# Two-layer hybrid encoder: fp32r weight halves made by casting and adding transfers instead of a raw copy and two engines

## The chip, the cores and the metric

The kernel runs on one core of a Trainium2 chip. The metric is the device time of one execution in microseconds; the profile shows one such execution, with TensorE (PE; PEld is its weight load), VectorE (DVE), ScalarE (ACT), GpSimd (POOL), SyncE (SP) and the 16 DMA engines of the core.

## The reference

Sizes: 512 tokens, width 1024, two layers, MLP width 2816, a memory of 256 tokens. Cut to what matters here, every layer is a chain of matrix products with weights that are read once:

```python
for i in range(DEPTH):
    h = rms_norm(x, attn_norm[i])
    if i % 2 == 0:
        proj = h @ w_in_diff[0]          # 1024 x 2560: q, k, v, memory queries
        mix = diff_attention(...)
    else:
        proj = h @ w_in_gla[0]           # 1024 x 2576: q, k, v, gates, memory queries
        mix = gla_attention(...)
    cross = memory_cross_attention(mem_q, mem, ..., w_mem_kv[i], ...)   # 1024 x 512
    x = x + concat(mix, cross) @ w_out[i]                              # 1024 x 1024
    h = rms_norm(x, ffn_norm[i])
    u = h @ w_up[i]                                                    # 1024 x 5632
    c = causal_depthwise_conv3(u) + conv_b
    a, g = split(c, 2)
    x = x + (silu(g) * a) @ w_down[i]                                  # 2816 x 1024
```

All inputs and outputs are fp32.

## The kernel before

The big products run on TensorE in the type fp32r, which holds fewer bits than fp32. So that the result keeps its accuracy, each fp32 operand is held as two fp32r tiles: `hi`, the operand rounded to fp32r, and `lo`, the rest (operand minus `hi`). A product is then three matmuls: hi by hi, hi by lo, lo by hi. Activations are split where they are made (`xsh`, `xsl`, `midh`, `midl`). The weights are split on the chip as they arrive, and the change is about that.

The host packs all weights into `wpack`, one block after another in the order of use. A block is 128 partitions by up to 1024 columns (`WTILE`), 512 KB when full. Several blocks make a piece (`_pieces`, `_blocks`). A projection piece of 512 output columns has four blocks (two row tiles of the weight in each); an "up" piece ("ua" or "ug": 256 columns of the one or the other half of `w_up`) has two; a "down" piece has three, in the second half of the MLP two and a half.

`make_piece` brings one piece: for each block SP loads it into one of three `raw` buffers (L207), ACT copies it with rounding into a `whi` tile (L200), and DVE subtracts that from the raw block into a `wlo` tile (L201). `whi` and `wlo` are rings of `WB` = 5 tiles each. `weights(key)` hands out the piece that comes next and makes sure that one piece ahead of it has been ordered. The first piece (`raw0` to `raw3`) and the second are brought in the opening section by loads written out by hand (L373, and `second`), with the same split.

TensorE's order is the order in which the program is written. The order on ACT, DVE, POOL and SP is chosen by a scheduler when the kernel is built, outside the opening section; each engine then works through its own list in that order and waits on semaphores.

Around the weights: `gemm` (L250 to L252) computes a projection, for each of four groups of 128 tokens over all blocks of the piece, and hands its units to the queue `F` (class `Filler`), which slips them between the steps of attention. `product` (L267 to L269) computes 128 output columns for all 512 tokens with the weights as the stationary operand. In `ffn` a round takes one "ua" and one "ug" piece and runs four products: ua, ug, ua, ug. In the first layer a product takes the row tiles in the order 4, 0, 5, 1, 6, 2, 7, 3 (from `tiles`), so that it reads both of its blocks by turns; in the second layer in the order 0 to 7. After each product DVE multiplies by the row scale (L1017), ACT and DVE do the convolution (L1019 to L1021), the silu and the split (L1047 to L1051). POOL has little to do: it fills corners of `bt` and the first columns of `u` (memsets, L606, L1005), and adds sums of squares (L335).

Of the kernel before, what the change touches and what calls it, by code (L numbers as in the profile page):

```python
# [10 lines left out]
F32 = mybir.dt.float32  # L11
# [3 lines left out]
ALU = mybir.AluOpType  # L15
# [13 lines left out]
WTILE = 1024  # L29
HALVES = (6, 5)  # L30
XS = 36
WB = 5
FA, FB = 3.0, 1.2
K8 = tuple(range(KT))
C4 = tuple(range(4))
# [93 lines left out]
def trunk(ctx, tc, x_t, mem_t, wpack, cols_a_d, cols_d, conv_d, gate_d, rel_bias, diff_lambda, consts, onehot, out):  # L129
    nc = tc.nc  # L130
    mm = nc.tensor.matmul
    V, A, G = nc.vector, nc.scalar, nc.gpsimd
# [3 lines left out]
    wp = ctx.enter_context(tc.tile_pool(name="wp", bufs=2))  # L136
# [5 lines left out]
    def bank(tag):  # L142
        return ps.tile([128, 512], F32, name=f"ps_{tag}", tag=tag)

    def xtile():
        return xs.tile([128, S], F32, name="xt", tag="xs", bufs=XS)

    def split_tiles(pool=None, tag="xs", bufs=XS):
        pool = pool or xs
        return (pool.tile([128, S], F32R, name=tag + "h", tag=tag, bufs=bufs),  # L150
                pool.tile([128, S], F32R, name=tag + "l", tag=tag, bufs=bufs))
# [4 lines left out]
    def blk(b, w=128):  # L156
        return slice(w * b, w * b + w)
# [39 lines left out]
    at = [0]  # L197

    def split_weights(c, raw, hi, lo):
        A.copy(hi[:, c], raw[:, c])  # L200
        V.tensor_sub(lo[:, c], raw[:, c], hi[:, c].bitcast(F32))  # L201

    def raw_tile():
        return wp.tile([128, WTILE], F32, name="raw", tag="raw", bufs=3)

    def load_raw(raw, n):
        nc.sync.dma_start(raw[:, :n], wpack[at[0], :, :n])  # L207
        at[0] += 1
        return raw

    def make_piece(raws=None):
        parts = []
        for i, (_, _, kk, _, w) in enumerate(blocks[len(made)]):
            n = len(kk)
            raw = load_raw(raw_tile(), n * w) if raws is None else raws[i]
            hi, lo = (wp.tile([128, WTILE], F32R, name=t, tag=t, bufs=WB) for t in ("whi", "wlo"))
            split_weights(slice(0, n * w), raw, hi, lo)
            parts += [(hi[:, blk(j, w)], lo[:, blk(j, w)]) for j in range(n)]
        made.append(parts)

# [2 lines left out]
    def weights(key):  # L223
        i = used[0]
        assert plan[i][0] == key, (plan[i][0], key)
        while len(made) < min(i + 2, len(plan)):
            make_piece()
        used[0] += 1
        parts, made[i] = made[i], None
        return parts  # L230

    def split(hi, lo, src, gain):
        A.activation(hi, src, AF.Copy, scale=gain)
        V.scalar_tensor_tensor(lo, src, gain, hi.bitcast(F32), op0=ALU.mult, op1=ALU.subtract)  # L234
# [76 lines left out]
    def bias_rows(rb, oh, bs):  # L311
        for c in (slice(0, 512), slice(512, 640)):
            n = c.stop - c.start
            p = bank("lg")
            mm(p[:6, :n], rb, oh[:, c], start=True, stop=True)
            V.tensor_copy(bs[c.start // 512], p[:6, :n])
# [14 lines left out]
    def squares(src, acc, eng=V):  # L331
        sq = xtile()
        A.activation(sq, src, AF.Square)
        if acc[0] is not None:
            eng.tensor_add(sq, sq, acc[0])  # L335
        acc[0] = sq

    def token_rsqrt(tag, sq, nb, y, on_dve=False):
        p = bank(tag)
        for b in range(nb):  # L340
            mm(p[:, b:b + 1], sq[:, blk(b)], ones[:, 0:1], start=True, stop=True)
        return rsqrt(p[:, :nb], nb, 1.0 / D, on_dve, y=y)

    def small_vectors():
        for c in (c_dq, c_mq(0), c_mq(1)):
            V.tensor_scalar_mul(c, c, 0.125)
        V.tensor_scalar_mul(c_do, c_do, 1.0 - LAM_INIT)
        for t in range(3):
            V.tensor_scalar_mul(c_go(t), c_go(t), 0.5)
        lam(lv, xtile()[:, 0:128].rearrange("p (a b) -> p a b", a=2))  # L350
# [3 lines left out]
    with tc.tile_pool(name="ini", bufs=1) as ip, tc.manual_schedule(engines={E.Activation, E.DVE, E.Pool, E.SP}):  # L354
        idle = ip.tile([128, 512], F32, name="idle")
        rb = ip.tile([32, 6], F32, name="rb")
        oh = ip.tile([32, 640], F32, name="oh")
        bs = xtile()[:6], xtile()[:6, :128]
        lv = xtile()[:, :256]
        G.memset(idle, 0.0)  # L360
        p = bank("tp")
        for n in (512, 320):
            mm(p[:, :n], idle[:, 0:128], idle[:, :n], start=True, stop=True)


        raws = [ip.tile([128, WTILE], F32, name=f"raw{i}") for i in range(4)]
        A.dma_start(raws[0][:, blk(0, S)], wpack[0, :, blk(0, S)])
        load(cols_a, cols_a_d)
        for k in range(KT):
            xT[k] = xtile()  # L370
            load(xT[k], x_t[k])
            if k:
                load(raws[k // 2][:, blk(k % 2, S)], wpack[k // 2, :, blk(k % 2, S)])  # L373
        at[0] = 4
        load(C[:, 640:768], consts[:, 640:768])
        load(rb, rel_bias)
        load(oh, onehot)
        second = [load_raw(raw_tile(), WTILE) for _ in range(3)]
        load(cols, cols_d)
        load(lv, diff_lambda[0].rearrange("a b -> (a b)").partition_broadcast(128))  # L380
        parts, acc, split_w = [], [None], [None]
        made.append(parts)

        def operands(k):
            if k % 2 == 0:
                split_w[0] = [wp.tile([128, WTILE], F32R, name=n, tag=n, bufs=WB) for n in ("whi", "wlo")]
            c = blk(k % 2, S)
            hi, lo = split_w[0]
            xh[k], xl[k] = split_tiles()
            if k == 0:  # L390
                V.tensor_copy(hi[:, c], raws[0][:, c])
                V.tensor_sub(lo[:, c], raws[0][:, c], hi[:, c].bitcast(F32))
                split(xh[0], xl[0], xT[0], c_attn(0, 0))
            else:
                split(xh[k], xl[k], xT[k], c_attn(0, k))
                split_weights(c, raws[k // 2], hi, lo)
            parts.append((hi[:, c], lo[:, c]))
            squares(xT[k], acc)

        operands(0)  # L400
        for k in range(KT):
            if k + 1 < KT:
                operands(k + 1)
            if k == 0:
                second.append(load_raw(raws[0], WTILE))
            if k == 4:
                bias_rows(rb, oh, bs)
            if k == KT - 2:
                make_piece(second)
                weights(("qk", 0))  # L410
                token_rsqrt("lg", acc[0], NB, r_x[:, 0])
                small_vectors()
                for c in range(2):
                    load(bias_d[:, 512 * c:min(512 * c + 512, 640)], bs[c])
            hi, lo = parts[k]
            terms = (xh[k], hi), (xh[k], lo), (xl[k], hi)
            todo = [(b, i) for b in range(NB) for i in range(3)]
            for b, i in sorted(todo, key=lambda bi: bi[1]) if k == 0 else todo:
                xp, w = terms[i]
                mm(first[b], xp[:, blk(b)], w, start=k == 0 and i == 0, stop=k == KT - 1 and i == 2)  # L420
# [736 lines left out]
```

## Time and profile before

| | |
|---|---|
| median of 3 runs | 1204.51 us (1204.1 to 1205.91) |
| profiled execution, time | 1205.31 us |
| profiled execution, span | 1203.5 us |
| TensorE busy | 1188.3 us (99%) |
| DVE busy | 759.8 us (63%) |
| ACT busy | 540.7 us (45%) |
| POOL busy | 23.5 us (2%) |
| read from HBM | 112.63 MB |
| granted TensorE clock | 1.0 |

The span runs from the first to the last instruction of the program; the execution's own time has some 2 us around it. Matmuls are pipelined and their ends are modelled, so a busy TensorE is not necessarily one at its peak. Rows name the operation by its line in the kernel, its engine and its tiles (out<-in); "idle before" is the time that the engine had waited, and "<-" names what ended that wait. A DMA's issue is a row of the queue that issues it (SPq), its landing is counted from there.

### The profile page before, as it was taken

Reading aid. Unit: us, or ns where it says so; the run is one execution under the profiler, and the core shown is the slowest. Engines: PE = TensorE matmul, PEld = TensorE weight load, DVE = VectorE, ACT = ScalarE, POOL = GpSimd, SP = SyncE. Lnnn points to the kernel's source line nnn. Section 1 sums busy time; section 2 is a strip of 40 time slices with the busy share of each in tenths; the row PEclk is TensorE's granted clock in tenths of the full one; section 3 lists DMA queues with packets and bytes.
Section 4 is the critical chain, followed back from the end, with each engine's and each line's share of the span. In section 5 each row is a group of like instructions: output and inputs, shape, how many; then the busy total and the mean of one; then the engine's idle time right before and its main releaser. Section 6 shows DMA issues by size and latency. Waiting matters only on the chain.

```text
span 1203.5 us, 14757 instructions
## 1 busy us (share of the span) xinstructions
PE 1188.3 (99%) x5672; PEld 975.0 (81%) x5672; DVE 759.8 (63%) x1259; ACT 540.7 (45%) x915; POOL 23.5 (2%) x37
## 2 busy tenths in 40 slices
PE   9999999999999999999999999999999999999998
PEld 6887777778888888888787888987888888888887
DVE  7566578887776534767546446768677653476741
ACT  6666666554444222434436444536444432243420
POOL 0000000000000000000020000003000000000000
PEclk9999999999999999999999999999999999999999
DMA  8432231232332331422342221234233233232231
GB/s 275 132 101 84 80 118 49 71 105 88 98 112 70 123 105 53 130 80 88 116 146 74 70 71 57 62 127 133 78 98 112 71 123 97 67 122 84 87 114 44
DMA packets 39413, 117.80 MB, mean 98 GB/s; under 512 B 4688, under 2 KB 5769, under 8 KB 39343
## 3 DMA queue, kind: packets, MB, share of 16 engines
q1 hardware_dynamic: 39198, 116.60, 30.5%
q8 instruction: 44, 0.72, 0.2%
q10 hardware_dynamic: 144, 0.26, 0.1%
q14 instruction: 27, 0.21, 0.1%
HBM read 112.63 MB, written 4.21 MB: 97 GB/s over the span
## 4 chain that ended last, share of the span: by engine, by line
PE 90%; DVE 5%; ACT 3%; issue 1%; DMA 1%; SPq 0%; DVEq 0%; ACTq 0%
PE ps_mm L268 8%; PE ps_mm L269 8%; PE ps_mm L267 8%; PE ps_sm L267 6%; PE ps_sm L268 6%; PE ps_sm L269 6%; PE ps_mm L250 6%; PE ps_mm L252 6%; PE ps_mm L251 5%; PE ps_tp L267 3%; PE ps_tp L268 3%; PE ps_tp L269 3%; PE ps_lg L268 3%; PE ps_lg L269 3%; PE ps_lg L267 3%; PE ps_tp L169 2%
## 5 line engine op out<-in xcount | busy, mean ns | idle before, releaser
L200 ACT CAST whi<-raw 128x1024 fp32r<-128x1024 f32 (+2 forms) x214 | 207.7, 976 | 247.5 <-PE ps_tp L268 133.8
L201 DVE TENSOR_TENSOR wlo<-raw,whi 128x1024 fp32r<-128x1024 f32 (+2 forms) x214 | 240.8, 1136 | 111.0 <-ACT whi L200 109.9
L267 PE MATMUL ps_mm<-xsh,whi 128*128 128x512 f32 x460 | 182.5, 397 | 0.2 <-DVE xt L969 0.2
L268 PE MATMUL ps_mm<-xsl,whi 128*128 128x512 f32 x460 | 179.4, 390 | 1.4 <-DVE xsl L234 1.3
L269 PE MATMUL ps_mm<-xsh,wlo 128*128 128x512 f32 x460 | 179.3, 390 | 0.0
L268 PE MATMUL ps_sm<-xsl,whi 128*128 128x512 f32 x372 | 144.7, 389 | 0.0
L267 PE MATMUL ps_sm<-xsh,whi 128*128 128x512 f32 x372 | 144.7, 389 | 0.0
L269 PE MATMUL ps_sm<-xsh,wlo 128*128 128x512 f32 x372 | 144.7, 389 | 0.0
L250 PE MATMUL ps_mm<-whi,xsh 128*128 128x512 f32 (+2 forms) x352 | 138.2, 393 | 0.1
L252 PE MATMUL ps_mm<-whi,xsl 128*128 128x512 f32 (+2 forms) x352 | 131.4, 373 | 0.3 <-DVE xsl L234 0.3
L251 PE MATMUL ps_mm<-wlo,xsh 128*128 128x512 f32 (+2 forms) x352 | 130.6, 371 | 0.0
L1019 ACT ACTIVATE cvo<-u,cv 128x512 f32<-128x512 f32 x88 | 71.6, 815 | 114.0 <-DVE u L1017 113.6
L268 PEld LDWEIGHTS ps_mm<-xsl,whi 128*128 128x128 f32 x460 | 86.5, 188 | 20.2 <-DVE xsl L234 2.7
L267 PEld LDWEIGHTS ps_mm<-xsh,whi 128*128 128x128 f32 x460 | 86.4, 188 | 18.2 <-DVE xt L969 0.9
L269 PEld LDWEIGHTS ps_mm<-xsh,wlo 128*128 128x128 f32 x460 | 86.3, 188 | 18.1
L1020 DVE SCALAR_TENSOR_TENSOR cvo<-u,cv,cvo 128x512 f32<-128x512 f32 x88 | 65.9, 749 | 31.6 <-ACT cvo L1019 31.4
L268 PEld LDWEIGHTS ps_sm<-xsl,whi 128*128 128x128 f32 x372 | 69.8, 188 | 14.6
L269 PEld LDWEIGHTS ps_sm<-xsh,wlo 128*128 128x128 f32 x372 | 69.8, 188 | 14.5
L267 PEld LDWEIGHTS ps_sm<-xsh,whi 128*128 128x128 f32 x372 | 69.8, 188 | 14.4
L252 PEld LDWEIGHTS ps_mm<-whi,xsl 128*128 128x128 f32 x352 | 66.1, 188 | 12.7 <-DVE xsl L234 0.5
L250 PEld LDWEIGHTS ps_mm<-whi,xsh 128*128 128x128 f32 x352 | 66.3, 188 | 10.7 <-issue 0.9
L251 PEld LDWEIGHTS ps_mm<-wlo,xsh 128*128 128x128 f32 x352 | 66.5, 189 | 9.5
(247 smaller groups left out, 1767.9 us busy)
## 6 DMA issues: line engine op xcount, KB each, us to landing
raw<-in_wpack_dram SPq DMA_DIRECT2D x176, 512.0 KB, 3.5
raw<-in_wpack_dram SPq DMA_DIRECT2D x27, 256.0 KB, 3.5
xt<-in_x_t_dram SPq DMA_DIRECT2D x16, 256.0 KB, 5.3
xres<-xt SPq DMA_DIRECT2D x8, 256.0 KB, 3.5
xt<-xres SPq DMA_DIRECT2D x8, 256.0 KB, 4.4
out_dram<-xt SPq DMA_DIRECT2D x8, 256.0 KB, 2.0
bt<-bias_d SPq DMA_DIRECT2D x6, 256.0 KB, 5.2
raw<-in_wpack_dram SPq DMA_DIRECT2D x4, 384.0 KB, 2.9
```

The lines of the kernel that those rows point to most:

```text
L169: nc.tensor.transpose(dst, src, ident[:n, :n])
L200: A.copy(hi[:, c], raw[:, c])
L201: V.tensor_sub(lo[:, c], raw[:, c], hi[:, c].bitcast(F32))
L250: mm(p, sh[k][:, blk(b)], hi, start=k == 0, stop=False)
L251: mm(p, sh[k][:, blk(b)], lo, start=False, stop=False)
L252: mm(p, sl[k][:, blk(b)], hi, start=False, stop=k == KT - 1)
L267: mm(p, hi[:, blk(n)], bh, start=i == first, stop=False)
L268: mm(p, hi[:, blk(n)], bl, start=False, stop=False)
L269: mm(p, lo[:, blk(n)], bh, start=False, stop=i == last)
L1019: A.activation(c, u[:, 2:], AF.Identity, scale=cv[l][:, 2, j:j + 1], bias=cv[l][:, 3, j:j + 1])
L1020: V.scalar_tensor_tensor(c, u[:, 1:S + 1], cv[l][:, 1, j:j + 1], c, op0=ALU.mult, op1=ALU.add)
```

## The change

A block is no longer loaded as it is. POOL issues a transfer from `wpack` into `whi` that rounds to fp32r on the way (fp32 to fp32r is a change of type, so the transfer casts). ACT writes the negative of `whi` into `wlo`. Then POOL issues a second transfer of the same block from `wpack` that adds to what stands in `wlo`, which leaves the weight minus `whi` there. So each such block is read from HBM twice, DVE has no part in it, and the `raw` buffers are gone from the ring pool. The rings of `whi` and `wlo` grow from five to six tiles. The first two pieces keep the former split; three of the raw tiles of the second piece now come from the opening section's pool, under names of their own. Nothing else is edited. Line numbers from L217 on shift by five.

```diff
-WB = 5
+WB = 6
...
-    def raw_tile():
-        return wp.tile([128, WTILE], F32, name="raw", tag="raw", bufs=3)
-
...
     def make_piece(raws=None):
         parts = []
         for i, (_, _, kk, _, w) in enumerate(blocks[len(made)]):
             n = len(kk)
-            raw = load_raw(raw_tile(), n * w) if raws is None else raws[i]
+            c = slice(0, n * w)
             hi, lo = (wp.tile([128, WTILE], F32R, name=t, tag=t, bufs=WB) for t in ("whi", "wlo"))
-            split_weights(slice(0, n * w), raw, hi, lo)
+            if raws is None:
+                G.dma_start(hi[:, c], wpack[at[0], :, c])
+                A.mul(lo[:, c], hi[:, c].bitcast(F32), -1.0)
+                G.dma_start(lo[:, c], wpack[at[0], :, c], accum_op=ALU.add)
+                at[0] += 1
+            else:
+                split_weights(c, raws[i], hi, lo)
             parts += [(hi[:, blk(j, w)], lo[:, blk(j, w)]) for j in range(n)]
         made.append(parts)
...
-        second = [load_raw(raw_tile(), WTILE) for _ in range(3)]
+        second = [load_raw(ip.tile([128, WTILE], F32, name=f"raw{4 + i}"), WTILE) for i in range(3)]
```

In the built program POOL holds 406 such transfers, 203 of each kind, in one list with its memsets and additions. An adding transfer waits there for ACT's copy, a rounding one for TensorE's last reading of the slot; whatever stands behind it in the list waits too.

## The prediction

> **What bounds the kernel now.** I read the page's busy times and chain first, then stretches of the span, then the weights' path, because the change touches nothing else.
>
> ```profile
> PE 1188.3 (99%) x5672; PEld 975.0 (81%) x5672; DVE 759.8 (63%) x1259; ACT 540.7 (45%) x915; POOL 23.5 (2%) x37
> ...
> PE 90%; DVE 5%; ACT 3%; issue 1%; DMA 1%; SPq 0%; DVEq 0%; ACTq 0%
> ```
>
> TensorE is busy for 1188.3 of 1203.5 us. Whatever is taken off VectorE (DVE) or ScalarE (ACT) can win at most what TensorE now idles, 1203.5 - 1188.3 = 15.2 us. The stretches (us, then busy time and count of instructions by engine, granted clock, DMA share, GB/s) say where that idle time is:
>
> ```profile
> 65.00:240.00 175.00, 170.72 (x981) 136.55 (x980) 125.70 (x334) 106.53 (x273) 0.58 (x4) 1.00 0.26 81
> 290.00:567.00 277.00, 277.00 (x1218) 228.31 (x1217) 171.09 (x214) 104.60 (x129) 0.00 (x0) 1.00 0.30 94
> 567.00:700.00 133.00, 129.66 (x671) 106.55 (x670) 69.04 (x118) 61.12 (x118) 10.53 (x11) 1.00 0.30 98
> ```
>
> In the first MLP (290 to 567) there is none: 277.00 / 1218 = 0.227 us from one matmul to the next, so a weight block of 24 matmuls feeds TensorE for 5.46 us, and a quarter block (6 matmuls) for 1.37. The two attention stretches idle for 4.3 and 3.3 us. So the kernel is bound by TensorE, and the question is whether weights still arrive in time. Now the path of a block:
>
> ```profile
> L201 DVE TENSOR_TENSOR wlo<-raw,whi 128x1024 fp32r<-128x1024 f32 (+2 forms) x214 | 240.8, 1136 | 111.0 <-ACT whi L200 109.9
> L200 ACT CAST whi<-raw x214: 404/1050/1095, 6.9 to 1181.6; 128x1024 fp32r<-128x1024 f32 x89, 128x512 fp32r<-128x512 f32 x15, 128x768 fp32r<-128x768 f32 x2, 128x816 fp32r<-128x816 f32 x1
> L207 SPq DMA_DIRECT2D raw<-in_wpack_dram x207: 327/328/587, 13.1 to 1169.2; - x104
> DMA to landing us min/median/max: 2.0/3.5/6.8
> ...
> SPq L207 <- DVE wlo L201: 867.5, 179, 27.6
> ...
> ACT whi L200 <- DMA raw<-in_wpack_dram: 6.6, 9, 4.4
> q1 hardware_dynamic: 39198, 116.60, 30.5%
> ```
>
> The first rows are group, form and landing times; the last three are two waits (us, times, longest) and the page's DMA queue. A 512 KB raw load lands 3.5 us after its issue, but nobody feels it: SP waits 867.5 us for raw buffers (the loads run three blocks ahead), and ACT waits only 6.6 us in the whole run for a load. After a slot of the ring comes free, only a 1.05 us cast and a subtraction stand between TensorE and the block. How tight that is, one round of the first MLP shows (start, duration):
>
> ```profile
> 302.77 2.00 ACT L200 CAST whi<-raw 128x1024 fp32r<-128x1024 f32 x2
> 307.72 2.26 ACT L200 CAST whi<-raw 128x1024 fp32r<-128x1024 f32 x2 [2.23 <-issue]
> ...
> 303.51 0.68 DVE L1017 TENSOR_TENSOR u<-ps_sm,rB 128x512 f32<-128x512 f32 x1
> 304.11 2.35 DVE L201 TENSOR_TENSOR wlo<-raw,whi 128x1024 fp32r<-128x1024 f32 x2
> 308.58 0.69 DVE L1017 TENSOR_TENSOR u<-ps_sm,rB 128x512 f32<-128x512 f32 x1 [0.68 <-PE ps_sm L269]
> 314.30 0.68 DVE L1017 TENSOR_TENSOR u<-ps_mm,rB 128x512 f32<-128x512 f32 x1
> ```
>
> Each L1017 follows the end of one product of 24 matmuls: the second "ua" product (about 303), the second "ug" (308.6), the first "ua" of the next pair (314.3). At 302.77 two slots come free, and at 304.11 + 2.35 = 306.46 both next "ug" blocks are ready, 3.7 us later. They are needed when the product that ends before 314.30 is over: 11.5 us after the release. So 7.8 us are to spare.
>
> **The change, part by part.**
>
> *Removed.* 203 subtractions (207 issues of L207 less the four of the second piece, which keeps the old path) of about 1.14 us, some 230 us of DVE. They lie beside matmuls; I take the gain at 0, and at most 15.2. On ACT the cast becomes a negative copy of the same size: 1.05 for 1.05, 0.
>
> *Added.* 203 rounding loads and 203 adding loads, all issued by POOL, whose order in the changed program is, once in step, W W L W L W L L for four blocks (W rounds, L adds). An L waits for ACT's copy, a W for TensorE to free the slot. What one costs no row shows. POOL's issue: above SP's 0.33 us (L207), below POOL's dearest operation,
>
> ```profile
> L335 POOL TENSOR_TENSOR xt<-xt 128x512 f32<-128x512 f32 x12 | 19.1, 1588 | 380.0 <-ACT xt L333 375.7 <-issue 3.7 <-POOL xt L335 0.4
> ```
>
> 1.59 us; I take the middle, 1.0. Landing of W after the issue: 3.5 - 0.33 = 3.2 us as for a raw load (range 1.7 to 6.5 from the landing row). Bytes: queue q1 moved 116.60 MB in 0.305 x 1203.5 = 367 us of all 16 engines, so 512 KB hold them 1.65 us. L fetches the old contents besides the weights, so I give it one pass more: 3.3 us of the engines, and landing 3.2 + 1.65 = 4.85 after the issue (range as fast as W, to twice that pass). Together 4.95 us of DMA per block against 5.46 us of matmuls: full, but not over.
>
> *Moved: the prefetch.* The raw buffers are gone. The load itself now waits for a ring slot, so 3.2 us of landing and the whole L come into the path that had 7.8 us to spare. First MLP, from the release (0): W1 issued 0 to 1, W2 1 to 2; W1 lands 4.2; copy done 5.25; L1 issued 5.25 to 6.25. Next on POOL is a W of the following pair, which needs the slot freed at 308.58 - 302.77 = 5.8: issued 6.25 to 7.25. L2: 7.25 to 8.25. It lands at 8.25 + 4.85 = 13.1 if the engines are free; queued behind L1 (to 9.55) and that W (to 11.2) its bytes end at 14.5 and it lands 14.5 + 1.55 = 16.05. The first half is read 0.45 us (two matmuls) before the second, so it is due at 11.95. Late by 1.15 to 4.1; the queue is really there, so 4.0. Ten pairs follow another in this layer: **40 us** (12 to 41).
>
> Second MLP: here a product reads its first block to the end before its second, so a block is freed half a product (2.7 us) before the other, or needed that much later. The second block then has 14.2 us instead of 11.5: late by nothing to 2. Ten rounds at 1: **10 us** (0 to 20).
>
> Down projections: pieces of three blocks (2.5 in the second half), two of which just fill the ring. A piece lasts 3 x 5.46 = 16.4 us; bringing three blocks holds the engines 14.9 us and ends some 1 + 1.55 later, 17.4, or less by the overlap of copies. 16 pieces at 1.5 late: **24 us** (0 to 40).
>
> Projections of the attention stretches: a piece is four blocks, all read by each of four row groups, so a ring of six holds the running piece and two blocks. The third block of the next piece gets its slot in the last row group, five quarter blocks before it is due, 5 x 1.37 = 6.85 us; it needs 4.2 + 1.05 + 5.85 = 11.1. The fourth comes 3.3 behind it and is due 1.37 later: 6.2 late. Some attention work lies between the quarters, so 5 for each of nine such pieces (five in the first layer, four in the second): **45 us** (0 to 56).
>
> ACT: it runs in order, and a negative copy at its head now waits for a landing. Behind it stand evacuations and exponentials for which TensorE waits. In the two attention stretches there are 27 + 45 such copies:
>
> ```profile
> L200 ACT CAST whi<-raw 128x1024 fp32r<-128x1024 f32 (+1 forms) x27 | 23.6, 873 | 8.4 <-PE ps_mm L252 4.3 <-PE ps_mm L268 3.6 <-DMA raw<-in_wpack_dram 0.4
> ...
> L200 ACT CAST whi<-raw 128x1024 fp32r<-128x1024 f32 (+5 forms) x45 | 41.6, 927 | 36.0 <-PE ps_mm L268 13.3 <-PE ps_tp L268 10.1 <-PE ps_mm L252 5.7
> ```
>
> Before, the first 27 waited 0.4 us for loads. A wait may reach 4.2 us; I take 0.75 each for what reaches TensorE: **55 us** (0 to 150). POOL's own few operations (memsets of bt and u, sums of squares) now stand among the transfers; bt's memset waits for its load and holds later L back, counted in the above.
>
> *Sum.* 40 + 10 + 24 + 45 + 55 = 174 us on the profiled execution's 1205.3 us: 1380. The median of the runs shown is 1204.5, 0.8 us less, which changes nothing here.
>
> **The rivals.**
>
> *The DMA engines become the bound.* If adding (or rounding) runs slower than a plain load per byte, W and L together pass 5.46 us per block and everything waits for transfers. For: 4.95 is close. Against: no row shows such a transfer. If L holds the engines 6.6 us (twice my value), 8.25 us x 190 full blocks (100 MB of packed weights) = 1570, and with the rest of the bytes (17 MB, about 50 us, half beside it) 1600 us.
>
> *The ring nearly covers it.* POOL issues in 0.33 us and L lands like a plain load. Then L2 is issued at 6.5 and lands near 9.8, before 11.95: no MLP loss. Projections lose (0.33 + 3.2 + 1.05 + 3.55 - 6.85) = 1.3 each, 12 us, and ACT 0.2 for each of 72 copies, 14: about 1231. For: loads were never felt before. Against: the lead of three raw blocks shrinks to one more ring slot.
>
> *Faster.* One mechanism: DVE's 230 us gone lets TensorE recover its idle time. It decides if every L lands before its due time and no copy waits, that is with W landing at the 2.0 us of the fastest raw load. For: 5% of the chain is DVE. Against: the MLP has nothing to recover. At most 1205.3 - 15.2 = 1190; I price it at 1196.
>
> *TensorE slows after its waits.* The granted clock is 1.00 in every stretch, and no stretch of before has TensorE idle for long, so the trace shows nothing of what a wait of 4 us does. If some 25 such waits are each followed by 12 matmuls at half the clock, that is 12 x 0.227 = 2.7 us each, 68 us more: 1448. The Trainium skill (TensorE: Matmul & The Clock Gate, "What's actually happening") says that about 3.4 us of idling halves the array's clock until about 3.4 us of activity; by that rule each costs some 1.7 us, an estimate of 1423. No run here shows it yet.
>
> **How the numbers follow.** Forecast 0.42 (its own range 1300 to 1480), engines bound 0.24, nearly covered 0.17, slowed clock 0.11, faster 0.06. The prediction is 1380. The low end 1225 takes in most of "nearly covered" and the lower bounds of the terms; the high end 1700 takes in an L somewhat dearer than 6.6 us; outside stay the faster case, some 0.04 of the nearly covered and 0.08 of the bound one, 0.18. Faster by over 0.2% (about what a measurement can tell from no change): 0.06; within it 0.02, the bottom of "nearly covered"; slower 0.92.
>
> **What would show it.** Right: TensorE idle in the first MLP's rounds of about 26 us instead of 21.8, waits of TensorE on "wlo" transfers, DVE without L201 but for the first two pieces, negative copies waiting for DMA. Engines bound: DMA share near 1 throughout. Nearly covered: TensorE still above 97%. Slowed clock: granted clock below 1. The sum is wrong if TensorE's waits lie mainly behind ACT in the MLPs, or if POOL's issues take much over 1 us, which would lengthen every chain three times.

## The result: 12.9% slower, and the profile after

The changed kernel takes 1358.7 us (median of four runs, 1357.14 to 1362.55) against 1204.3 us (1203.64 to 1205.91) for the kernel before: ratio 1.1285, 95% interval 1.1258 to 1.1311. The profiled execution took 1357.14 us, with a span of 1355.4 us and a granted clock of 0.962.

The page after, in its busy times, its DMA queue of POOL (packets, MB, share of 16 engines) and its chain by engine:

```profile
PE 1242.4 (92%) x5672; PEld 1004.7 (74%) x5672; DVE 548.6 (40%) x1056; ACT 542.6 (40%) x915; POOL 307.6 (23%) x443
...
q0 software_dynamic: 58464, 197.29, 65.7%
...
issue 50%; PE 21%; POOL 15%; DMA 10%; ACT 2%; DVE 1%; POOLq 0%; SPq 0%; ACTq 0%
```

The first row divides the loss. The same 5672 matmuls are busy 1242.4 - 1188.3 = 54.1 us longer, and TensorE idles 1355.4 - 1242.4 = 113.0 us instead of 15.2, which is 97.8 us more. Together 151.9, the whole growth of the span. In the chain PE has gone from 90% to 21%. POOL and DMA make a quarter of it, and half is what the profile calls issue, time in which an engine waited for nothing that it shows. DVE lost 211 us of work and nothing came of it.

What TensorE waits for (us in total, times, longest), largest first:

```profile
PE ps_mm L274 <- DMA wlo<-in_wpack_dram: 36.7, 10, 5.5
PE ps_mm L256 <- DMA wlo<-in_wpack_dram: 32.7, 12, 5.5
PE ps_lg L272 <- ACT midh L1055: 10.4, 4, 4.5
```

L274 is the MLP's product and L256 the projection. Adding transfers that land late account for 69.4 of the 97.8 us; the other 28.4 are inputs that ACT and DVE finish late, the third row the largest of them. Stage by stage (us, then busy times of PE, PEld, DVE, ACT and POOL, granted clock, DMA share, GB/s), the two kernels cut at the same instructions; first the kernel before:

```profile
65.00:240.10 175.10, 170.82 (x982) 136.61 (x981) 125.74 (x335) 106.63 (x273) 0.58 (x4) 1.00 0.26 81
274.20:394.10 119.90, 119.90 (x531) 99.28 (x530) 87.53 (x112) 54.77 (x68) 0.00 (x0) 1.00 0.29 89
394.10:467.60 73.50, 73.50 (x320) 59.84 (x319) 26.84 (x29) 16.68 (x17) 0.00 (x0) 1.00 0.36 114
467.60:571.00 103.40, 103.40 (x457) 85.60 (x457) 72.47 (x94) 44.26 (x56) 0.00 (x0) 1.00 0.27 85
620.10:830.20 210.10, 207.33 (x1149) 177.89 (x1148) 130.58 (x257) 100.37 (x194) 5.61 (x12) 1.00 0.27 86
848.80:968.00 119.20, 119.20 (x527) 98.75 (x526) 89.32 (x114) 55.65 (x69) 0.00 (x0) 1.00 0.31 96
```

and the kernel after:

```profile
71.20:283.90 212.70, 184.90 (x981) 144.45 (x981) 104.97 (x310) 107.06 (x275) 38.13 (x58) 0.93 0.52 119
326.20:473.30 147.10, 129.46 (x531) 104.56 (x530) 63.93 (x90) 53.44 (x66) 29.54 (x42) 0.94 0.67 150
473.30:548.30 75.00, 74.16 (x321) 59.79 (x319) 9.13 (x14) 16.49 (x18) 18.72 (x27) 1.00 0.79 183
548.30:679.70 131.40, 112.33 (x458) 90.62 (x457) 53.38 (x76) 46.24 (x57) 28.04 (x40) 0.94 0.68 151
732.10:965.30 233.20, 215.16 (x1149) 181.90 (x1148) 97.57 (x222) 97.53 (x190) 52.18 (x79) 0.97 0.62 140
990.10:1109.30 119.20, 119.20 (x527) 98.76 (x526) 62.47 (x90) 54.18 (x68) 30.27 (x43) 1.00 0.83 185
```

The rows are, in order: attention of the first layer (+37.6 us), the rounds of the first half of the first MLP (+27.2), its down projection (+1.5), the rounds of the second half (+28.0), attention of the second layer (+23.1), and the rounds of the first half of the second MLP, but for their beginning (0.0). That last row is worth a second look: the DMA share is highest there, 0.83, and TensorE idles for nothing. It runs the same kind of rounds as the second row, which lost 27 us at a share of 0.67. So over a whole round of the rows that lose, the DMA engines are not the bound; they are waiting too.

One round of the first MLP shows on what. POOL's issues, ACT's negative copies and the matmul that waits (start, duration, idle before in brackets):

```profile
386.85 1.22 POOL L217 DMA_DIRECT2D whi<-in_wpack_dram  x2 [8.19 <-PE ps_sm L274]
392.06 0.87 POOL L219 DMA_DIRECT2D wlo<-in_wpack_dram  x1 [3.98 <-ACT wlo L218]
392.61 0.87 POOL L217 DMA_DIRECT2D whi<-in_wpack_dram  x1
393.36 1.02 POOL L219 DMA_DIRECT2D wlo<-in_wpack_dram  x1
```

```profile
390.70 1.06 ACT L218 ACTIVATE wlo<-whi 128x1024 fp32r<-128x1024 f32 x1 [1.20 <-DMA whi<-in_wpack_dram]
392.00 1.06 ACT L218 ACTIVATE wlo<-whi 128x1024 fp32r<-128x1024 f32 x1 [0.24 <-PE ps_sm L273]
```

```profile
402.19 0.50 PE L274 MATMUL ps_mm<-xsh,wlo 128*128 128x512 f32 x1 [3.40 <-DMA wlo<-in_wpack_dram]
```

POOL idles 8.19 us until TensorE frees the slots at 386.85. Both rounding loads go out at once, the copies follow at 390.70 and 392.00, the adding loads at 392.06 and 393.36, with a rounding load of the following pair between them. The second block can be read at 402.19, that is 15.34 us after the release; it was due at 402.19 - 3.40 = 398.79, 11.94 after it. The same round by stretches, before the release, in the wait and just behind it:

```profile
382.60:386.80 4.20, 4.20 (x20) 3.50 (x19) 2.34 (x4) 1.60 (x3) 0.00 (x0) 1.00 0.00 0
398.85:402.10 3.25, 0.00 (x0) 0.00 (x0) 1.19 (x2) 1.56 (x2) 0.86 (x1) 1.00 1.04 247
402.90:406.20 3.30, 3.30 (x10) 2.53 (x9) 0.88 (x2) 1.76 (x2) 0.86 (x1) 0.50 0.72 140
```

The DMA engines move nothing until the slots come free and are full in the wait: the round's transfers are pressed into what is left of it, and part of the 15.34 us is their own queue. Behind the wait the granted clock is 0.50, and the matmuls start 0.43 us apart instead of 0.23 until about 406.1.

### The profile page after: what moved, and what is told of

It reads as the page before. It is cut to its first block, busy times and chain, and to the rows that moved or that the text cites. A ratio compares the mean times of both kernels' runs of the same rounds, so it can differ in the third digit from the quotient of the medians.

```text
span 1355.4 us, 14877 instructions
## 1 busy us (share of the span) xinstructions
PE 1242.4 (92%) x5672; PEld 1004.7 (74%) x5672; DVE 548.6 (40%) x1056; ACT 542.6 (40%) x915; POOL 307.6 (23%) x443
## 4 chain that ended last, share of the span: by engine, by line
issue 50%; PE 21%; POOL 15%; DMA 10%; ACT 2%; DVE 1%; POOLq 0%; SPq 0%; ACTq 0%
POOL wlo L219 7%; POOL whi L217 7%; DMA whi<-in_wpack_dram 5%; DMA wlo<-in_wpack_dram 4%; PE ps_mm L256 1%; PE ps_mm L257 1%; PE ps_mm L255 1%; PE ps_tp L273 1%; PE ps_tp L272 1%; PE ps_tp L274 1%; PE ps_sm L273 1%; PE ps_lg L273 1%; PE ps_sm L272 1%; PE ps_mm L274 1%; PE ps_lg L274 1%
## 5 line engine op out<-in xcount | busy, mean ns | idle before, releaser
L218 ACT ACTIVATE wlo<-whi 128x1024 fp32r<-128x1024 f32 (+4 forms) x203 | 201.7, 996 | 432.8 <-DMA whi<-in_wpack_dram 413.1
L219 POOL DMA_DIRECT2D wlo<-in_wpack_dram x203 | 178.0, 884 | 565.5 <-ACT wlo L218 512.0
L217 POOL DMA_DIRECT2D whi<-in_wpack_dram x203 | 136.9, 678 | 416.9 <-PE ps_sm L274 151.5
L274 PE MATMUL ps_mm<-xsh,wlo 128*128 128x512 f32 x460 | 189.5, 412 | 36.7 <-DMA wlo<-in_wpack_dram 36.7
L272 PE MATMUL ps_mm<-xsh,whi 128*128 128x512 f32 x460 | 191.9, 417 | 4.3 <-DVE xt L974 2.9
L273 PE MATMUL ps_mm<-xsl,whi 128*128 128x512 f32 x460 | 188.3, 409 | 2.0 <-DVE xsl L239 2.0
L256 PE MATMUL ps_mm<-wlo,xsh 128*128 128x512 f32 (+2 forms) x352 | 138.3, 393 | 32.7 <-DMA wlo<-in_wpack_dram 32.7
L255 PE MATMUL ps_mm<-whi,xsh 128*128 128x512 f32 (+2 forms) x352 | 143.7, 408 | 1.5 <-ACT rr L749 1.0
L274 PE MATMUL ps_sm<-xsh,wlo 128*128 128x512 f32 x372 | 144.7, 389 | 0.0
L274 PEld LDWEIGHTS ps_mm<-xsh,wlo 128*128 128x128 f32 x460 | 91.6, 199 | 60.9 <-DMA wlo<-in_wpack_dram 40.9
L272 PEld LDWEIGHTS ps_mm<-xsh,whi 128*128 128x128 f32 x460 | 91.8, 200 | 25.2 <-DVE xt L974 3.3
L256 PEld LDWEIGHTS ps_mm<-wlo,xsh 128*128 128x128 f32 x352 | 69.7, 198 | 48.9 <-DMA wlo<-in_wpack_dram 39.1
L274 PEld LDWEIGHTS ps_sm<-xsh,wlo 128*128 128x128 f32 x372 | 69.8, 188 | 14.5
```

Source lines behind the costliest of these rows:

```text
L217: G.dma_start(hi[:, c], wpack[at[0], :, c])
L218: A.mul(lo[:, c], hi[:, c].bitcast(F32), -1.0)
L219: G.dma_start(lo[:, c], wpack[at[0], :, c], accum_op=ALU.add)
L255: mm(p, sh[k][:, blk(b)], hi, start=k == 0, stop=False)
L256: mm(p, sh[k][:, blk(b)], lo, start=False, stop=False)
L272: mm(p, hi[:, blk(n)], bh, start=i == first, stop=False)
```

## The experiments

The theory, from here on "lead": the loss is the series of slot free, rounding load, copy, adding load, which now begins only when a slot of the ring comes free. The rivals: the DMA engines as the bound ("throughput"), ACT held up by copies that wait at the head of its list, and TensorE's clock. Medians are of four runs, and beside them the kernel before took 1205.5 to 1205.6 us.

**Order of the row tiles.** In the first layer, from the second round on, a product reads its first block to the end before its second, as the second layer does. Nothing else of the weights' path is touched.

```diff
-            product(p, parts, n, list(zip(xh, xl)), order)
+            product(p, parts, n, list(zip(xh, xl)), order if i < 4 else K8)
```

> Only the first layer's MLP from its second round on takes the row tiles in the order 0 to 7, as the second layer does, so that a product finishes its first block before it reads its second. Bytes, transfers and queues are as in the changed kernel. If the loss is a lack of lead (theory), the 55 us of the first MLP's rounds (27.3 us a round instead of 21.8) go almost wholly: about 1305 us, rounds of 21.8 to 22.5. If the DMA engines are the bound (rival), nothing changes: 1350 to 1360.

Measured 1307.4 us, ratio 1.0839 (1.0805 to 1.0872): 51 less than after. The two stretches of rounds:

```profile
325.00:446.00 121.00, 120.47 (x531) 99.12 (x530) 61.90 (x88) 52.55 (x66) 29.84 (x43) 1.00 0.80 183
525.30:629.70 104.40, 103.88 (x458) 85.37 (x457) 52.55 (x76) 44.39 (x56) 26.34 (x39) 1.00 0.84 189
```

The same bytes now pass in 121.0 and 104.4 us instead of 147.1 and 131.4, and the clock is back at 1.00. Throughput as the bound of a whole round is refuted for the first MLP, and all but 2 us of its 55 are lead, with what follows a wait.

**The second transfer left out, or made plain.** First L219 is deleted, so that `wlo` stays at minus `whi`; then L219 stays but overwrites `wlo` instead of adding, so that both halves hold the weight. Both keep ACT's copies and their waits.

```diff
-                G.dma_start(lo[:, c], wpack[at[0], :, c], accum_op=ALU.add)
```

> The adding transfer is left out, so wlo holds the negative of whi and the result lacks the low half of the weights. Theory: a block then needs 0.55 us of issue, about 4 us of landing and a copy of 1.06, some 6 us, less than the 11.5 of the first MLP and less than the 6.85 of the projections: 1215 to 1235. Rival (ACT waiting at the head of its list for the rounding load is what costs): these waits stay, and the time stays above 1280.

```diff
-                G.dma_start(lo[:, c], wpack[at[0], :, c], accum_op=ALU.add)
+                G.dma_start(lo[:, c], wpack[at[0], :, c])
```

> The second transfer stays, at the same place, waits for the same copy and casts, but does not add, so wlo holds the rounded weights and the result is off. If the adding itself is dear (its engine time 3.3 us by the prediction against 1.65), its landing falls from 5.7 us towards 5.0 or less, the share of the software queue from 65.7% to about 45%, and the time to 1310 to 1335. If the cost lies in the second transfer as such, 1345 to 1360.

Without it 1215.77 us, ratio 1.0094 (1.0073 to 1.0116); with a plain one 1250.1, ratio 1.0385 (1.0354 to 1.0416). Of the 154 us, 143 hang on the second transfer, as its theory had it, and 109 on its adding, more than either expectation had given it (1310 at the lowest). The queue and the landing times (x, KB, median us from issue) without it:

```profile
q0 software_dynamic: 29232, 98.64, 27.0%
...
whi<-in_wpack_dram POOLq DMA_DIRECT2D x172, 512.0 KB, 3.8
```

with a plain one, and POOL's issues (count, min/median/max in ns):

```profile
q0 software_dynamic: 58464, 197.29, 51.0%
...
wlo<-in_wpack_dram POOLq DMA_DIRECT2D x172, 512.0 KB, 3.8
```

```profile
L219 POOL DMA_DIRECT2D wlo<-in_wpack_dram x203: 530/530/576, 32.9 to 1219.7; - x102
```

and after:

```profile
whi<-in_wpack_dram POOLq DMA_DIRECT2D x172, 512.0 KB, 5.0
wlo<-in_wpack_dram POOLq DMA_DIRECT2D x172, 512.0 KB, 5.7
```

```profile
L217 POOL DMA_DIRECT2D whi<-in_wpack_dram x203: 527/554/1225, 25.9 to 1323.8; - x102
...
L219 POOL DMA_DIRECT2D wlo<-in_wpack_dram x203: 833/862/1212, 32.9 to 1329.5; - x102
```

98.64 MB are 188.1 blocks of 512 KB. A rounding load holds the engines 0.270 x 1214.2 / 188.1 = 1.74 us, and rounding and plain loads together 0.510 x 1246.0 / 376.2 = 1.69 us each. With the adding load a block takes 0.657 x 1355.4 / 188.1 = 4.73 us. Adding also lengthens POOL's issue from 0.53 to 0.86 us and the landing from 3.8 to 5.7.

**The copy on DVE.** The negative copy moves from ACT to DVE (0.69 us there); built so, POOL's list in the MLPs becomes W W L L, without the next pair's W between the two L.

```diff
-                A.mul(lo[:, c], hi[:, c].bitcast(F32), -1.0)
+                V.tensor_scalar(lo[:, c], hi[:, c].bitcast(F32), -1.0, None, op0=ALU.mult)
```

> The negative copy is made by VectorE instead of ACT; the transfers are the same, though the scheduler puts them as W W L L on POOL in the MLPs instead of W W L W L W L L. If ACT's waiting at the head of its list costs the attention stretches much (55 us in the prediction's sum), they get 20 to 50 us shorter. If the path of the block is what counts, the attention stretches change by under 10 us.

Measured 1336.59 us, ratio 1.1086 (1.1059 to 1.1113). Attention of the first and of the second layer:

```profile
71.20:273.10 201.90, 178.33 (x982) 140.52 (x981) 114.73 (x329) 85.16 (x244) 38.84 (x58) 0.96 0.55 126
...
690.30:936.80 246.50, 222.93 (x1149) 188.78 (x1148) 116.57 (x257) 71.56 (x160) 56.21 (x81) 0.92 0.59 135
```

10.8 us shorter, and 13.3 longer: neither expectation. The gain lies in the first MLP (18.3 us in the rounds of its first half, some 13 in those of the second), where POOL's order changed too. This does not bear out ACT's waiting as a great cost; copies that wait on DVE seem to cost as well.

**Order and copy together.**

> e1 (row tiles in order in the first MLP) and e4 (negative copy on VectorE) together; alone they took 51 and 22 us off. If both shorten the same wait of the first MLP's rounds, e4 adds little: 1295 to 1310. If they act on different waits, the gains add: about 1285.

1331.68 us, ratio 1.1055 (1.1016 to 1.1094): neither expectation, and 24 above the order alone. Attention of the second layer stays long (240.3 us; 231.5 with the order alone), and the second MLP's first rounds go from 119.2 to 122.6. DVE waits 344.2 us with copies at its head in this run. How much of the 24 us is that, and how much POOL's other order, the two edits do not separate.

**Useless matmuls in the wait.** In the first MLP, ahead of the first "ug" product of each round but the very first, TensorE runs 14 matmuls whose result nobody reads. They fill some 3.2 us in which it would idle.

```diff
+                    if n == 0 and q and l == 0:
+                        pw = bank("tp")
+                        for _ in range(14):
+                            mm(pw, xh[0][:, 0:128], xh[0], start=True, stop=True)
```

> The changed kernel with 14 matmuls without use (3.2 us) put ahead of the first ug product of ten rounds of the first MLP, into the 3.4 us in which TensorE otherwise waits for the adding transfer. If the wait alone costs (rival), the time stays: 1355 to 1362. If the granted clock falls to one half for 3.4 us after each such wait (theory, 1.7 us each), the rounds go from 27.3 to about 25.6 and the time falls by about 17 us, to 1342; the clock events of those rounds are gone.

Measured 1342.51 us, ratio 1.1129 (1.1092 to 1.1166), 16.2 less than after, although TensorE does more work. Its waits, and the rounds of the first half, cut at the same instructions as the row of 147.10 us after (69 more matmuls are useless ones):

```profile
PE ps_mm L274 <- DMA wlo<-in_wpack_dram: 8.0, 12, 1.4
```

```profile
319.20:460.10 140.90, 137.29 (x600) 112.03 (x599) 64.30 (x91) 54.23 (x67) 29.49 (x42) 1.00 0.69 159
```

The blocks come no earlier; the waits on them fell from 36.7 to 8.0 us because the useless matmuls stand in their place, and the clock is 1.00 instead of 0.94. The five waits of this stretch give back 6.2 us. By the medians the clock costs 1.6 us for each of the ten waits. In the stretch after of 147.10 us with clock 0.94, 0.06 x 147.1 / 0.5 = 17.7 us ran at half speed, some 3.5 for each of the five rounds in it. The same for the whole span, 0.038 x 1355.4 / 0.5 = 103 us, of which half is lost, gives 51.5 of the 54.1 us by which TensorE is busy longer.

The Trainium skill (TensorE: Matmul & The Clock Gate, "What's actually happening") states halving after about 3.4 us of idling, undone by about 3.4 us of activity. The traces agree with the second half, some 3.4 us at half speed after such a wait, but not with 3.4 us as the measure of what starts it. After a wait of 3.42 us at 605.9 in the changed kernel the clock stays (first row); in the run with one raw buffer, told of below, it falls after two waits of 0.83 and 0.79 us (the other rows):

```profile
609.40:616.20 6.80, 6.80 (x30) 5.64 (x31) 2.21 (x4) 2.50 (x3) 0.86 (x1) 1.00 0.89 169
```

```profile
350.51 0.50 PE L267 MATMUL ps_mm<-xsh,whi 128*128 128x512 f32 x1 [0.83 <-ACT whi L200]
352.04 0.54 PE L269 MATMUL ps_mm<-xsh,wlo 128*128 128x512 f32 x1 [0.79 <-DVE wlo L201]
...
352.45:355.70 3.25, 3.25 (x9) 2.57 (x8) 1.55 (x3) 0.14 (x1) 0.00 (x0) 0.50 0.44 161
```

**One more block of ring.** Seven tiles instead of six; to make room, the pool of activation tiles shrinks from 36 to 34, and that alone is run beside it.

```diff
-XS = 36
-WB = 6
+XS = 34
+WB = 7
```

> The changed kernel with rings of seven blocks instead of six, paid for with two tiles of the pool xs (34 instead of 36). In the first MLP the first block of each ug piece no longer waits for the release, and in the projections three blocks of the next piece can be brought ahead. If lack of lead makes the loss: 1280 to 1320. If the engines' throughput does: 1345 to 1360.

> The changed kernel with 34 tiles in xs and the ring still at six, to tell how much of e9 is due to the smaller pool: expected within 10 us of the changed kernel's 1358.7.

1305.22 us, ratio 1.0844 (1.0784 to 1.0904), and with the smaller pool alone 1355.51, ratio 1.1237 (1.1177 to 1.1297). One block more of lead is worth 50 us, with not a byte less to move. In the two profiled executions (1316.62 and 1345.08 us) the gain lies in the first MLP, whose rounds go from 146.7 to 126.8 and from 126.8 to 112.6 us. The attention stretches stay as they are, 205.1 for 203.6 and 226.6 for 229.7 us, though their waits on adding transfers are shorter (11.9 us for 24.6). So the pair shows lead as the cause in the first MLP; for the attention stretches it does not show it.

**The old split with one raw buffer.** The old path, ring of six, but one raw buffer instead of three: is it the lost lead alone?

```diff
+        return wp.tile([128, WTILE], F32, name="raw", tag="raw", bufs=1)
```

> The old kernel's split by ACT and VectorE with one raw buffer instead of three and a ring of six. If losing the lead of the raw buffers is in itself what costs, it is slower by 3% or more (1240 up). Theory: only the lead together with a long path costs; a load of 3.5 us, a cast and a subtraction follow each other at some 6 us per block against 5.46 of matmuls, so 1210 to 1240.

1322.6 us, ratio 1.0961 (1.0939 to 1.0983): a miss, by far too much, on the side where the expectation had put the lost lead in itself. The first rounds of the second MLP, where the changed kernel loses nothing:

```profile
921.10:1056.50 135.40, 124.40 (x527) 99.48 (x526) 87.94 (x110) 55.13 (x67) 0.00 (x0) 0.98 0.25 82
```

22 blocks in 135.4 us are 6.15 us per block, with the DMA engines a quarter busy. One buffer puts load, cast and subtraction of every block in series, which is longer than the 5.46 us that a block feeds TensorE; 190 x 0.69 = 131 us. The 6 us that the expectation names would already have made 190 x 0.54 = 103 us, so its range did not follow from its own figure. This is a bound of its own and says nothing on the ring's lead.

**Only the rounding by transfer.** SP loads three raw blocks ahead as before, POOL's rounding load fills `whi`, DVE subtracts; ring of five.

```diff
+                raw = load_raw(wp.tile([128, WTILE], F32, name="raw", tag="raw", bufs=3), n * w)
+                G.dma_start(hi[:, c], wpack[at[0] - 1, :, c])
+                V.tensor_sub(lo[:, c], raw[:, c], hi[:, c].bitcast(F32))
```

> The first half of the change alone: whi by a rounding load from POOL, wlo by VectorE from a raw block that SP loads as before (three raw buffers, ring of five). Both blocks of an ug piece would be ready about 0.55 x 2 + 4.5 + 1.1 to 2.3 = 7 to 8 us after their release, before the 11.5 of the first MLP, and the projections late by 0 to 2 us a piece: 1210 to 1235. If any POOL transfer in the path ruins it, over 1270.

1258.71 us, ratio 1.043 (1.0413 to 1.0448): a miss, between the two expectations. One wait says where it went:

```profile
DVE wlo L219 <- DMA whi<-in_wpack_dram: 195.4, 109, 6.0
```

DVE stands 195.4 us with a subtraction at its head that waits for a landing. TensorE's own waits on weights are 3 us in this run, but it idles 1264.1 - 1215.2 = 48.9 us instead of 15.2, nearly all the rest on late results of DVE and ACT, and it is busy 1215.2 - 1188.3 = 26.9 us longer, at a granted clock of 0.98. So what I had charged to ACT in the prediction seems to exist, on DVE; no run takes DVE's waits alone away.

**Only the adding transfer.** Raw blocks as before, `whi` cast from them by ACT, then the negative copy and the adding load; ring of five. And the same with the raw loads left out, `whi` being cast from one fixed block.

```diff
+                raw = load_raw(wp.tile([128, WTILE], F32, name="raw", tag="raw", bufs=3), n * w)
+                A.copy(hi[:, c], raw[:, c])
                 A.mul(lo[:, c], hi[:, c].bitcast(F32), -1.0)
+                G.dma_start(lo[:, c], wpack[at[0] - 1, :, c], accum_op=ALU.add)
```

> The second half of the change alone: raw blocks loaded ahead by SP (three buffers, ring of five), whi cast by ACT, then ACT's negative copy and the adding transfer. A block is ready 1.05 + 1.06 + 0.86 + 4.9 = 7.9 us after its release, the second of a pair about 10 to 11: before 11.95 in the first MLP, 1 to 4 us late in each projection piece. Theory: 1225 to 1265. If the adding transfer alone makes the loss: over 1300.

```diff
-                raw = load_raw(wp.tile([128, WTILE], F32, name="raw", tag="raw", bufs=3), n * w)
+                raw = kon
```

> Like e8, but the raw loads are left out: every whi is cast from one fixed block, so the result is off, and the adding transfer is nearly the only traffic. By the engine time of e8's software queue (2.9 us per full block) and a landing of a rounding load of 3.8 with 1.74 of engine time in e2, an adding transfer alone lands about 5 us after its issue. Theory A (the adding transfer's own landing and engine time make the loss): the time stays above 1290. Theory B (it is slow because the raw loads stand in the same 16 engines; it landed 8.6 us after issue in e8): the landing falls to about 5 us and the time to 1225 to 1270.

With raw loads 1354.67 us, ratio 1.1236 (1.1219 to 1.1253), without them 1268.0, ratio 1.0513 (1.0492 to 1.0535). The queues and the landings with them:

```profile
q0 software_dynamic: 29232, 98.64, 39.9%
q1 hardware_dynamic: 39198, 116.60, 24.9%
...
raw<-in_wpack_dram SPq DMA_DIRECT2D x176, 512.0 KB, 7.0
wlo<-in_wpack_dram POOLq DMA_DIRECT2D x172, 512.0 KB, 8.6
```

and the queue and the landing without them:

```profile
q0 software_dynamic: 29232, 98.64, 44.1%
...
wlo<-in_wpack_dram POOLq DMA_DIRECT2D x172, 512.0 KB, 5.5
```

An adding load holds the engines 0.441 x 1269.4 / 188.1 = 2.98 us and lands 5.5 us after its issue. Beside a stream of loads that need not be early, it lands after 8.6, and these loads take 7.0 instead of 3.5. Beside each other, neither holds the engines longer (0.399 x 1351.7 / 188.1 = 2.87 us for an adding load, and q1's packets 0.249 x 1351.7 = 337 us, 367 before): so they seem to stand behind each other. The first run alone would have read as "adding by itself makes the whole loss". With its copy and its issue it makes 62 us; the other 87 of its 149 go with the raw loads in flight. They are not the casts' own waits: in the run with raw loads ACT waits for such a landing only once, for 4.6 us, in the opening section.

## Why the prediction was right, and which of its terms were not

**Direction and size.** 1380 stood against 1358.7, inside the forecast's own range of 1300 to 1480. The likeliest case, that the series behind a ring slot is the bound, is what the order of the row tiles and the seventh block showed for the first MLP. For the attention stretches, 37.6 + 23.1 = 60.7 us of the loss, it is argued from the waits on adding transfers and not shown.

**Removed work: nothing gained.** As said; DVE fell to 548.6 us and TensorE idles more.

**Prices of the transfers.** POOL's issue was put at 1.0 us and takes 0.55 (L217) and 0.86 (L219). The prediction counted a landing from the end of the issue, the profile counts it from the start. So rounding alone lands after 3.8 - 0.53 = 3.3 us instead of 3.2; adding after 5.5 - 0.86 = 4.6 instead of 4.85, and it holds the engines 2.98 instead of 3.3. Per block 4.73 instead of 4.95. But for POOL's issue, each is right within a tenth.

**First MLP, 40 us.** Due at 11.95 after the release, measured 11.94; ready at 16.05 with the queue, measured 15.34, and the engines were full in the wait; waits 36.7 us in ten. This step was right. But the rounds lost 55.2 us, because TensorE is busy (129.46 + 112.33) - (119.90 + 103.40) = 18.5 us longer in them: the clock.

**Second MLP, 10 us.** Measured 0.0 in the rounds shown, the low end of its bound.

**Down projections, 24 us.** Measured in all four some 15 us (75.0 for 73.5 in the one shown), yet none of it in waits on weights: 10.4 us are the row of `midh`, ACT late with the last activations. Before the longest of these waits two copies stood at ACT's head for landings, 4.36 and 2.36 us (at 1293.41 and 1297.53). Inside its bounds, but for a wrong reason: the engines' fixed order rather than the filling of the ring.

**Projections, 45 us.** The waits on weights at L256 are 32.7 us, about a quarter less.

**ACT's order, 55 us.** The worst term. It was meant for the two attention stretches, in which TensorE idles 27.8 and 18.0 us after the change. Its waits on weights there, and ACT's waits in the whole run:

```profile
PE ps_mm L256 <- DMA wlo<-in_wpack_dram: 17.9, 6, 5.5
...
PE ps_mm L256 <- DMA wlo<-in_wpack_dram: 11.0, 5, 4.4
...
ACT wlo L218 <- DMA whi<-in_wpack_dram: 413.1, 157, 10.3
```

The rest, 9.9 and 7.0 us, was 4.3 and 2.8 before: 9.9 us more, or 0.14 for each of 72 copies. ACT does stand 413.1 us with copies at its head, but little of it reaches TensorE, and with only the rounding load before the copy the whole kernel loses 10 us. The step that failed is the 0.75 us for each copy.

**The sum and the clock.** By cause: weights 69.4, late inputs 28.4, clock 54.1. The terms of the sum, all of them waits, came to 174 where the waits are 97.8; of the 76 us too much the clock, which the sum left out, made good 54.1. That is luck. It stood among the rivals at 68 us by 25 waits of 2.7, with an estimate of 1.7 each beside it; the useless matmuls gave 1.6. So forecast and clock rival came true together, and the total is nearer than its parts deserve. They should not have been rivals: whoever forecasts waits of 4 us forecasts what follows them.

**The other rivals.** Engines bound: refuted for the MLPs by the order of the row tiles and by the stretch at a share of 0.83 without a wait; in the attention stretches their share is 0.52 and 0.62. Nearly covered: that is the kernel with a plain second load, 1250 instead of the 1231 worked out; adding is what separates it from the result. Faster: no version shown here comes below the kernel before, in which TensorE has 15 us to give.

## What to carry to other kernels

When a prefetch buffer is given up, count the lead that it was: everything between the release of the ring slot and the last landing now has to fit before the block is due, and the order in which a product reads its blocks, or one more slot, moves that by as much as any engine's work (51 and 50 us here). Before a subtraction is replaced by an adding transfer, price it as 1.7 times a plain one on the DMA engines and look at what else will be in flight. And where waits of TensorE are forecast, add what the clock takes after them: here some 1.6 us for each wait of about 3.4.

## What the runs showed of the hardware

An adding load from HBM holds the engines 2.98 us per 512 KB where a rounding or plain second load takes 1.7, and its issue holds POOL 0.86 us instead of 0.53. Rounding on the way costs the engines next to nothing: 1.74 us, against 1.65 for a raw load. Two queues hurt each other at mean shares of 39.9% and 24.9% over the span: adding loads land after 8.6 us beside SP's raw loads and after 5.5 without them. The granted clock fell to 0.50 for some 3.4 us after a wait of 3.40 us, but also after two of 0.83 and 0.79 us. And a useless matmul can pay: 140 of them, in ten waits, gave back 16 us.
